# One step of a by-hand exponential moves between VectorE and GpSimd in an attention kernel

## The chip, the cores and the metric

The kernel runs on one core of one Trainium2 chip. The time is device time in microseconds (us) of one execution. A core has five engines with a queue each: TensorE (PE, matrix products; PEld are its weight loads), VectorE (DVE), ScalarE (ACT), GpSimd (POOL) and SyncE (SP, which here issues transfers only). Each works through its own queue in order, and they wait for each other by semaphores. An instruction that waits holds up all that stand behind it in its queue.

## What is computed

Attention with grouped heads: 8 batches, 512 positions, 32 query heads in 8 groups of 4 that share a key and a value head, 64 columns per head.

```python
scores = np.einsum('bhqd,bhkd->bhqk', Q, K_expanded) * scale
weights = np.exp(scores - np.max(scores, axis=-1, keepdims=True))
weights = weights / (np.sum(weights, axis=-1, keepdims=True) + 1e-10)
output = np.einsum('bhqk,bhkd->bhqd', weights, V_expanded)
```

## The kernel before

**Jobs.** The work is cut into 64 jobs (`NJOB`), one for each batch and key head. A job has two pairs of query heads (`NPAIR`), and for each pair 4 blocks of 128 keys by 2 heads: 16 blocks of 128 keys by 512 queries. For each block TensorE makes the transposed scores in PSUM (`scores`, L283), an engine takes the exponential into the float16 tile `pt`, and TensorE multiplies `pt` with V (`pv`, L376), whose 65th column of ones gives the sum of the weights. `norm` (L418, L423) takes the reciprocal `inv` of that sum and multiplies it into the output tile `o_sb`, which SP stores. The scores aren't shifted by their maximum; sums and values are checked for range, and a general path behind the fast one runs if a check fails.

**Who takes the exponential.** ScalarE does most blocks, two at a time (`act_tile`, L301, 128x1024). VectorE and GpSimd do `taken(j)` blocks of each job by hand: three in the jobs for which `WIDE(j)` holds (`j >= 4 and j % 4 < 3`, so three jobs running, then one with two blocks). In a three-block job ScalarE is left with 13 blocks: six full tiles and a half tile, which comes as the fifth. From job 4 on the jobs thus run in groups of four: a first, a middle and a last three-block job, then a two-block job. There are 15 such groups; the last one ends in job 63, which takes one block by hand.

**The exponential by hand.** Five instructions:
- `u` (L312, VectorE): scores times a factor plus an offset, rounded to int16, so that the bits are those of a float16 near the exponential. Two blocks come first, the third in a part of its own, one job ahead (`exp_d`).
- `f` (L324, VectorE): the ten mantissa bits of `u`.
- `g` (L329, `factor` in `exp_d2`): (f + a) * b. This is the correction's first step.
- `w` (L335, `product`, GpSimd): g times f, the correction itself.
- `pt` (L348, `exp_d4`, VectorE): u + w, in bits the weight. It is called in the next job.

Where `g` runs is set by `odd` in `exp_d2`. Before, `odd` holds for the middle and the last three-block job: there g is VectorE's, in all other jobs GpSimd's. In the middle one `exp_d2` returns g and w as `rest`, which the job's loop calls further down, behind the third `u` of the next job; in the last one g is issued at once, behind f and ahead of the copy of the transposes.

**Order of a job** (the loop over j from 1 to 62, by hand, no scheduler): ScalarE tile 0, first `u`, tile 1, pv of the previous job's first pair in two halves with tile 2 between, `norm`, tile 3; then the half tile and the transposes of the queries of job j + 2 (L215) in the two banks of a fresh `d_ps`; `exp_d4` of the previous job; `exp_d2` of this one; the copy of the transposes (`qt`, L220); pv of the previous job's second pair in parts between tiles 5 and 6, with the third `u` of the next job; `rest`; `norm`. Every engine sees its own instructions in that order.

**Buffers.** PSUM has two `s_ps` tiles for ScalarE's scores, one `d_ps` (scores for VectorE, or transposes) and one `pv`. So pv of a pair can start only when `o_sb` of the pair before has read `pv`, and the next `s_ps` scores stand behind it in TensorE's queue. `u`, `f`, `g`, `w` have two buffers each. GpSimd also issues the loads of Q, K and V (L114 to L142), at the start of a job; the first and the two-block jobs have some, the middle and the last none.

Of the kernel before, what the change touches and what calls it, by code (L numbers as in the profile page):

```python
# [40 lines left out]
WIDE = lambda j: j >= 4 and j % 4 < 3  # L41
# [26 lines left out]
def fast_path(ctx, tc, Q, K, V, out, flag, ident):  # L68
# [78 lines left out]
    def d_tile():  # L147
        return d_pool.tile([128, 2, S], FP32, name="d_ps")
# [3 lines left out]
    def first_k(gp, swap, bank):  # L152
        half_bank = bank.bitcast(BF16)[:, 0:S]
        ps = half_bank.rearrange("p (sc c) -> p sc c", sc=SC)
        h = 2 * gp
        done = []
        for sc in range(SC):
            if swap:
                for half, g in ((0, 1), (64, 0)):
                    done.append(nc.tensor.transpose(  # L160
                        ps[half:half + 64, sc, :], kn[0][:, sc, h + g, :], ident
                    ))
            else:
                done.append(nc.tensor.transpose(ps[:, sc, :], kn[0][:, sc, h:h + 2, :], ident))
        return done, lambda: nc.vector.tensor_copy(
            out=kt_first[:, gp, swap, :], in_=half_bank
        )
# [22 lines left out]
    def dma_k(b, lo=0):  # L190
        kt[b] = kt_pool.tile([128, 2, GP, S], BF16, name="kt")
        for sc in range(SC):
            nc.sync.dma_start_transpose(
                out=kt[b][:, 0, lo:, sc * 128:(sc + 1) * 128],
                in_=kn[b][:, sc, 2 * lo:, :].rearrange("p g d -> p (g d)"),
            )
        for to, of in ((0, 64), (64, 0)):
            nc.sync.dma_start(out=kt[b][to:to + 64, 1, lo:, :], in_=kt[b][of:of + 64, 0, lo:, :])
# [27 lines left out]
    def piece(bank, done, read):  # L226
        copy = read()
        for other, written, taken_out in pieces:
            if other != bank:
                for this in done:  # L230
                    apart(this, taken_out)
                for before in written:
                    apart(copy, before)
        pieces.append((bank, done, copy))

    def check_v(b, sc):
        n = b * SC + sc
        nc.vector.tensor_reduce(  # L238
            out=okv[:, n:n + 1], in_=vt[b % 2][:, sc, :, 0:D], op=ALU.max, axis=AX.XY,
            apply_absolute_value=True,  # L240
        )
# [4 lines left out]
    def taken(j):  # L246
        return 1 if j == NJOB - 1 else 3 if WIDE(j) else 2
# [14 lines left out]
    for b in range(B):  # L262
        span = range(max(3, 8 * b + 1), min(8 * b + 9, NJOB - 3))
        two = [j for j in span if not WIDE(j)]
        odd = [j for j in span if WIDE(j) and not WIDE(j + 1)]
# [25 lines left out]
    def open_job(j):  # L291
        pt = pt_pool.tile([128, NPAIR, SC, 2, S], FP16, name="pt")
        jobs.setdefault(j, {}).update(pt=pt, pv={})

    def act_tile(j, n, spare=None):
        group = act_tiles(j)[n]
        i, kc, lo = group[0]
        ps = s_pool.tile([128, 2, S], FP32, name="s_ps") if spare is None else spare
        for _, _, m in group:
            scores(j, ps[:, m, :], i, kc, m)  # L300
        return nc.scalar.activation(  # L301
            out=jobs[j]["pt"][:, i, kc, lo:, :], in_=ps[:, lo:, :], func=EXP, scale=scale
        )

    def exp_d(j, lo, hi, ps, other=None):
        st = jobs.setdefault(j, {})
        if "u" not in st:
            for name, dtype in (("u", I16), ("f", I16), ("g", BF16), ("w", BF16)):
                st[name] = dve_pool.tile([128, 3, S], dtype, name=name + "16")[:, 0:taken(j), :]
        for n in range(lo, hi):  # L310
            apart(scores(j, ps[:, n - lo, :], DPAIR, *divmod(d_block(j) + n, 2)), other)
        return lambda: nc.vector.tensor_scalar(  # L312
            out=st["u"][:, lo:hi, :], in0=ps[:, 0:hi - lo, :], scalar1=A_U, scalar2=B_U,
            op0=ALU.mult, op1=ALU.add,
        )
# [3 lines left out]
    def exp_d2(j, engine=None):  # L319
        st = jobs[j]  # L320
        by_bits = engine is None
        engine = engine or nc.gpsimd
        odd = WIDE(j) and WIDE(j - 1)
        nc.vector.tensor_single_scalar(  # L324
            out=st["f"], in_=st["u"], scalar=1023, op=ALU.bitwise_and
        )

        def factor():
            (nc.vector if odd else engine).tensor_scalar(  # L329
                out=st["g"], in0=st["f"], scalar1=-EXP_F1,  # L330
                scalar2=EXP_K * 2.0 ** (24 * by_bits), op0=ALU.add, op1=ALU.mult,
            )

        def product():
            engine.tensor_tensor(  # L335
                out=st["w"], in0=st["g"], in1=st["f"].bitcast(FP16) if by_bits else st["f"],
                op=ALU.mult,
            )

        if odd and WIDE(j + 1):  # L340
            return lambda: (factor(), product())
        factor()
        return product() if by_bits else product
# [20 lines left out]
    def pv(j, i, lo, hi):  # L364
        st = jobs[j]
        u, g = divmod(j, 2)
        b, gp = divmod(u, GP)
        if lo == 0:

            t = d_tile() if (j, i) == (NJOB - 1, 0) else pv_tile()  # L370
            t = t.rearrange("p m (qc c) -> p m qc c", qc=SC)
            st["pv"][i] = t[:, :, :, 0:D + 1]
        order = blocks(j, i)
        for n in range(lo, hi):
            kc, m, qc = order[n]
            nc.tensor.matmul(  # L376
                st["pv"][i][:, m, qc, :],
                st["pt"][:, i, kc, m, qc * 128:(qc + 1) * 128],
                vt[b % 2][:, kc, 2 * gp + g, :],
                start=(n < 2 * SC and qc == 0),  # L380
                stop=(n >= len(order) - 2 * SC and qc == SC - 1),
            )
# [11 lines left out]
    def check_sums():  # L394
        while full:
            k, n = full.pop()
            cols = n * 2 * SC
            flat = invs.pop(k).rearrange("p s m qc -> p (s m qc)")[:, 0:cols]
            in_bounds((ok[:, 0:cols], ok[:, 0:cols]), flat, ok[:, 0:cols])
# [161 lines left out]
    act_tile(0, 3)  # L561
    act_tile(0, 4)
    exp_d2(0)
    bank = pv_tile()
    piece(0, *trans_q(1, bank[:, 0, :], 0, 1))
# [6 lines left out]
    for j in range(1, NJOB - 1):  # L572
        last = j - 1
        u, g = divmod(j, 2)
        b, gp = divmod(u, GP)
        open_job(j)
        if j == 1:
            nc.gpsimd.tensor_copy(out=gate, in_=jobs[0]["pt"][0:1, 0, SC - 1, 0, 0:1])
        for load, *of in LOADS.get(j, ()):
            load(*of)  # L580
        if j == 1:
            dma_k(0, 2)
        if gp == 2 and g == 0 and b + 1 < B:
            dma_k(b + 1)

        cut = (11, 19) if taken(j) < 3 else (4, 18) if taken(last) < 3 else (4, 16)
        act_tile(j, 0)
        if j == 1:
            piece(1, *first_k(1, 0, bank[:, 1, S // 2:]))
        exp_d(j, 0, 2, d_tile())()  # L590
        act_tile(j, 1)
        if j < 4 or j % 4 == 0:
            check_sums()
        if (j, 0) in CHECKS:
            check_v(*CHECKS[j, 0])
        pv(last, 0, 0, 16)
        act_tile(j, 2)
        pv(last, 0, 16, 32)
        norm(last, 0)
        act_tile(j, 3)  # L600

        reads = []
        bank = d_tile()
        beside = act_tile(j, 4, bank) if taken(j) > 2 else None

        ahead = (j + 1,) if j < 2 else (3, 4) if j == 2 else (j + 2,)
        for n, to in enumerate(ahead):
            if to < NJOB:
                reads.append(trans_q(to, bank[:, n, :], other=beside)[1])
        if j == 1:  # L610
            reads.append(first_k(1, 1, bank[:, 1, :])[1])
        exp_d4(last)
        rest = exp_d2(j)
        copies = [read() for read in reads]
        if taken(j) == 2:
            act_tile(j, 4)
        pv(last, 1, 0, cut[0])
        act_tile(j, 5)
        if beside:
            pv(last, 1, *cut)  # L620
        if taken(j + 1) > 2:
            exp_d(j + 1, 2, taken(j + 1), bank[:, 1:2, :], copies[0])()
        if rest:
            rest()
        if (j, 1) in CHECKS:
            check_v(*CHECKS[j, 1])
        if not beside:
            pv(last, 1, *cut)
        act_tile(j, 6)
        pv(last, 1, cut[1], 32)  # L630
        norm(last, 1)
        del jobs[last]

    j, last = NJOB - 1, NJOB - 2
# [144 lines left out]
```

## Time and profile before

| | us |
|---|---|
| median of 3 runs | 410.0 (409.52 to 410.16) |
| the profiled execution | 410.13 |
| its span, first to last instruction | 408.3 |
| ScalarE busy | 397.2 |
| TensorE busy | 374.7 |
| VectorE busy | 370.2 |
| GpSimd busy | 257.4 |

The granted TensorE clock was 0.998 of full speed. In the timeline's lines the first number is the start in us from the beginning of the span, the second the length in us; then come the engine, the line of the kernel, the operation, the tile written and the tiles read, shapes, and how many instructions were merged into the line. In square brackets stands the idle time of the engine just before, and what ended it. The records of one engine overlap a little, since the next instruction is taken up before the last result has landed, so lengths can't simply be added; starts and ends can be compared. Records of GpSimd are rough.

### The profile page before, as it was taken

To read this page: it belongs to the slowest core of one execution; us is meant where nothing else is said; L and a number is where in the kernel's file an instruction comes from. 1 tells how busy PE (TensorE), PEld (TensorE's weight loads), DVE (VectorE), ACT (ScalarE), POOL (GpSimd) and SP (SyncE) were. 2 spreads that over 40 slices of the span, in tenths; PEclk is the share of its full clock that TensorE was granted. 3 is DMA by queue.
4 is the path that set the end of the run, shared out by engine and by line. 5 is a ranking of instruction groups with operands and counts; after the bars stand their busy time and mean duration, and the time that the engine had idled before them with its cause. 6 is when DMAs were issued, how large, how long until landed. Compare 5 with 4: busy or idle time off the path is not lost.

```text
span 408.3 us, 13010 instructions
## 1 busy us (share of the span) xinstructions
PE 374.7 (92%) x5670; PEld 228.2 (56%) x5670; DVE 370.2 (91%) x653; ACT 397.2 (97%) x455; POOL 257.4 (63%) x151
## 2 busy tenths in 40 slices
PE   7999999998999999999998999999999999999975
PEld 3565565564655655555555555555555555555543
DVE  3788999999999998999989999899999999899985
ACT  5999999999999999999999999999999999999995
POOL 9858476675666666485674766567475684565552
PEclk9999999999999999999999999999999999999999
DMA  9989999699955999289890999919996399322205
GB/s 144 158 199 181 128 289 214 185 141 133 285 152 147 148 251 178 106 178 133 268 217 36 212 107 293 219 63 182 153 258 177 119 127 215 114 104 104 105 18 195
DMA packets 82893, 67.73 MB, mean 166 GB/s; under 512 B 52752, under 2 KB 57872, under 8 KB 82832
## 3 DMA queue, kind: packets, MB, share of 16 engines
q0 software_dynamic: 45072, 24.91, 62.1%
q1 hardware_dynamic: 37216, 41.75, 37.3%
q8 instruction: 45, 0.74, 0.8%
q10 hardware_dynamic: 544, 0.20, 0.2%
q14 instruction: 16, 0.13, 0.1%
HBM read 50.33 MB, written 33.55 MB: 205 GB/s over the span
## 4 chain that ended last, share of the span: by engine, by line
DVE 40%; PE 30%; ACT 27%; issue 3%; ACTq 0%; DVEq 0%
ACT pt L301 27%; PE pv L376 15%; DVE o_sb L423 11%; PE s_ps L283 11%; DVE u L312 6%; DVE pt L348 6%; DVE qt L220 5%; DVE g L329 4%; DVE inv L418 2%; DVE okv L238 2%; PE d_ps L215 2%; DVE f L324 2%; PE d_ps L283 1%; PE s_ps L512 1%; DVE inv_last L418 0%
## 5 line engine op out<-in xcount | busy, mean ns | idle before, releaser
L301 ACT ACTIVATE pt<-s_ps 128x1024 f16<-128x1024 f32 x403 | 381.3, 1094 | 2.5 <-PE s_ps L283 1.9
L335 POOL TENSOR_TENSOR w<-g,f 128x1536 bf16<-128x1536 bf16 (+1 forms) x63 | 177.4, 2816 | 88.8 <-DVE g L329 86.1
L376 PEld LDWEIGHTS <-pt 128*128 128x128 f16 x4096 | 142.4, 98 | 89.0 <-issue 42.9
L376 PE MATMUL pv<-v,pt 128*128 128x65 bf16 x4064 | 179.3, 195 | 10.9 <-DVE o_sb L423 10.1
L283 PE MATMUL s_ps<-qt,kt 64*128 64x512 bf16 x751 | 152.6, 384 | 9.0 <-ACT pt L301 7.2
L312 DVE TENSOR_SCALAR u<-d_ps 128x1024 int16<-128x1024 f32 (+1 forms) x109 | 107.8, 989 | 0.3
L423 DVE TENSOR_TENSOR o_sb<-pv,inv 128x512 f32<-128x512 f32 x121 | 83.6, 691 | 4.2
L283 PEld LDWEIGHTS <-kt 64*128 64x128 bf16 x960 | 50.0, 93 | 53.3 <-issue 29.3
L329 POOL TENSOR_SCALAR g<-f 128x1024 bf16<-128x1024 int16 (+1 forms) x33 | 40.6, 1230 | 53.3 <-DVE f L324 53.3
L283 PE MATMUL d_ps<-qt,kt 64*128 64x512 bf16 x209 | 56.9, 376 | 5.9 <-DVE qt L220 2.3
L348 DVE TENSOR_TENSOR pt<-u,w 128x1536 uint16<-128x1536 int16 (+1 forms) x64 | 55.3, 864 | 0.0
L418 DVE RECIPROCAL inv<-pv 128x8 f32<-128x8 f32 x121 | 24.8, 205 | 19.5 <-PE pv L376 17.4
L220 DVE COPY qt<-d_ps 128x1024 bf16<-128x1024 bf16 x62 | 42.2, 682 | 0.0
L215 PEld LDWEIGHTS <-q_nat 128*128 128x128 bf16 x508 | 28.5, 97 | 23.2 <-issue 23.2
L215 PE MATMUL d_ps<-ident,q_nat 128*128 128x128 bf16 x496 | 38.3, 221 | 0.0
L324 DVE TENSOR_SCALAR f<-u 128x1536 int16<-128x1536 int16 (+1 forms) x64 | 32.7, 512 | 0.0
L301 ACT ACTIVATE pt<-d_ps 128x512 f16<-128x512 f32 x45 | 31.0, 688 | 0.0
L238 DVE TENSOR_REDUCE okv<-v 128x1 f32<-128x512 bf16 x32 | 21.6, 675 | 0.0
L329 DVE TENSOR_SCALAR g<-f 128x1536 bf16<-128x1536 int16 (+1 forms) x31 | 16.9, 546 | 0.6
L142 POOL DMA_DIRECT2D q_nat<-in_Q_dram x19 | 15.4, 812 | 0.1
L283 PE MATMUL s_ps<-qt,kt_first 64*128 64x512 bf16 x56 | 11.1, 399 | 1.8 <-ACT pt L301 1.6
L127 POOL DMA_DIRECT2D v<-in_V_dram x7 | 12.3, 1759 | 0.0
(58 smaller groups left out, 55.1 us busy)
## 6 DMA issues: line engine op xcount, KB each, us to landing
out_dram<-o_sb SPq DMA_DIRECT2D x31, 1024.0 KB, 5.8
q_nat<-in_Q_dram POOLq DMA_DIRECT2D x14, 1024.0 KB, 11.5
k_nat<-in_K_dram POOLq DMA_DIRECT2D x7, 512.0 KB, 7.6
v<-in_V_dram POOLq DMA_DIRECT2D x7, 512.0 KB, 14.6
kt<-kt SPq DMA_DIRECT2D x14, 256.0 KB, 4.3
q_nat<-in_Q_dram POOLq DMA_DIRECT2D x3, 512.0 KB, 7.8
out_dram<-o_sb SPq DMA_DIRECT2D x4, 256.0 KB, 2.2
kt<-k_nat SPq DMA_TRANSPOSE x32, 10.3
```

The costliest lines, as they stand in the source:

```text
L215: nc.tensor.transpose(ps[:, i, sc, :], qn[u // 2][:, sc, h:h + 2, :], ident),
L220: return done, lambda: apart(nc.vector.tensor_copy(out=qt[u][:, g, lo:hi, :], in_=ps[:, lo:hi, :, :].rearrange("p i sc c -> p i (sc c)")), ...
L283: return nc.tensor.matmul(ps, keys[64 * m:64 * m + 64, g if u == 0 else g ^ m, kc * 128:(kc + 1) * 128], qt[u][64 * m:64 * m + 64, g, i, : ...
L301: return nc.scalar.activation(out=jobs[j]["pt"][:, i, kc, lo:, :], in_=ps[:, lo:, :], func=EXP, scale=scale)
L312: return lambda: nc.vector.tensor_scalar(out=st["u"][:, lo:hi, :], in0=ps[:, 0:hi - lo, :], scalar1=A_U, scalar2=B_U, op0=ALU.mult, op1=AL ...
L324: nc.vector.tensor_single_scalar(out=st["f"], in_=st["u"], scalar=1023, op=ALU.bitwise_and)
L329: (nc.vector if odd else engine).tensor_scalar(out=st["g"], in0=st["f"], scalar1=-EXP_F1, scalar2=EXP_K * 2.0 ** (24 * by_bits), op0=ALU.a ...
L335: engine.tensor_tensor(out=st["w"], in0=st["g"], in1=st["f"].bitcast(FP16) if by_bits else st["f"], op=ALU.mult,)
L348: nc.vector.tensor_tensor(out=st["pt"][:, DPAIR, :, :, :].rearrange("p kc m q -> p (kc m) q")[:, d_block(j):d_block(j) + n, :].bitcast(U16 ...
L376: nc.tensor.matmul(st["pv"][i][:, m, qc, :], st["pt"][:, i, kc, m, qc * 128:(qc + 1) * 128], vt[b % 2][:, kc, 2 * gp + g, :], start=(n < 2 ...
L418: nc.vector.reciprocal(out=inv, in_=sums[:, :, :, D:D + 1])
L423: nc.vector.tensor_tensor(out=osb[u][:, :, h:h + 2, :].rearrange("p qc m d -> p m qc d"), in0=sums[:, :, :, 0:D], in1=inv[:, :, :, None].t ...
```

## The change

g moves to GpSimd in the middle three-block job, at once behind f, with w behind it. In the last three-block job it stays on VectorE, but behind the copy of the transposes. `rest` is called directly behind the copies.

```diff
@@ exp_d2
-        odd = WIDE(j) and WIDE(j - 1)
+        odd = WIDE(j) and not WIDE(j + 1)
...
-        if odd and WIDE(j + 1):
+        if odd:
             return lambda: (factor(), product())
         factor()
         return product() if by_bits else product
@@ the loop over the jobs
         rest = exp_d2(j)
         copies = [read() for read in reads]
+        if rest:
+            rest()
         if taken(j) == 2:
             act_tile(j, 4)
         pv(last, 1, 0, cut[0])
...
         if taken(j + 1) > 2:
             exp_d(j + 1, 2, taken(j + 1), bank[:, 1:2, :], copies[0])()
-        if rest:
-            rest()
         if (j, 1) in CHECKS:
```

## The prediction

> **What bounds the kernel now.** I read the page's busy table first, then the timeline of each engine over one period of four jobs (204 to 230 us; by the first and last run of the sum below, 42.25 and 362.50 in 13 steps, it repeats every 24.6 us), and the waits noted in it.
>
> ```profile
> PE 374.7 (92%) x5670; PEld 228.2 (56%) x5670; DVE 370.2 (91%) x653; ACT 397.2 (97%) x455; POOL 257.4 (63%) x151
> ```
>
> ScalarE (ACT) has nearly no idle time. So the question is whether it runs at its own rate throughout. Its timeline, merged into runs of full tiles (x6, x13) and half tiles (x1), answers that; columns are start, length, engine, line:
>
> ```profile
> 208.60 0.71 ACT L301 ACTIVATE pt<-d_ps 128x512 f16<-128x512 f32 x1
> 209.07 5.73 ACT L301 ACTIVATE pt<-s_ps 128x1024 f16<-128x1024 f32 x6
> 214.53 0.77 ACT L301 ACTIVATE pt<-d_ps 128x512 f16<-128x512 f32 x1
> 215.00 5.94 ACT L301 ACTIVATE pt<-s_ps 128x1024 f16<-128x1024 f32 x6
> 220.84 0.59 ACT L301 ACTIVATE pt<-d_ps 128x512 f16<-128x512 f32 x1
> 221.31 12.03 ACT L301 ACTIVATE pt<-s_ps 128x1024 f16<-128x1024 f32 x13
> ```
>
> The records overlap, so I count from end to end. The half tile ends at 209.31 and the six tiles behind it at 214.80: 5.49 us, 0.915 each. The 13 tiles from 221.43 to 233.34 take 11.91, 0.916 each. That is ScalarE's own rate. The six between them, from 215.30 to 220.94, take 5.64: **0.15 us is lost, once in four jobs**, in the run that goes from the middle to the last of the three three-block jobs. TensorE (PE) shows what came late:
>
> ```profile
> 217.18 0.39 PE L283 MATMUL s_ps<-qt,kt 64*128 64x512 bf16 x2
> 217.96 0.67 PE L376 MATMUL pv<-v,pt 128*128 128x65 bf16 x16 [0.38 <-DVE o_sb L423]
> 218.56 0.39 PE L283 MATMUL s_ps<-qt,kt 64*128 64x512 bf16 x2
> ```
>
> TensorE works in order. Its pv matmuls wait 0.38 us for VectorE's (DVE) division o_sb, which empties the one pv buffer, and the next scores (218.56) stand behind them. VectorE is one unbroken queue there:
>
> ```profile
> 213.98 0.95 DVE L348 TENSOR_TENSOR pt<-u,w 128x1536 uint16<-128x1536 int16 x1
> 214.85 0.55 DVE L324 TENSOR_SCALAR f<-u 128x1536 int16<-128x1536 int16 x1
> 215.31 0.68 DVE L220 COPY qt<-d_ps 128x1024 bf16<-128x1024 bf16 x1
> 215.91 0.68 DVE L312 TENSOR_SCALAR u<-d_ps 128x512 int16<-128x512 f32 x1
> 216.51 0.55 DVE L329 TENSOR_SCALAR g<-f 128x1536 bf16<-128x1536 int16 x1
> 216.98 0.20 DVE L418 RECIPROCAL inv<-pv 128x8 f32<-128x8 f32 x1
> 217.21 0.69 DVE L423 TENSOR_TENSOR o_sb<-pv,inv 128x512 f32<-128x512 f32 x1
> ...
> 220.44 0.95 DVE L348 TENSOR_TENSOR pt<-u,w 128x1536 uint16<-128x1536 int16 x1
> 221.31 0.55 DVE L324 TENSOR_SCALAR f<-u 128x1536 int16<-128x1536 int16 x1
> 221.89 0.56 DVE L329 TENSOR_SCALAR g<-f 128x1536 bf16<-128x1536 int16 x1
> ...
> 223.20 0.69 DVE L423 TENSOR_TENSOR o_sb<-pv,inv 128x512 f32<-128x512 f32 x1
> ...
> 226.40 0.95 DVE L348 TENSOR_TENSOR pt<-u,w 128x1536 uint16<-128x1536 int16 x1
> ```
>
> The f at 214.85 is the middle job's, the one at 221.31 the last's. g is the step that the change moves: in the middle job it stands directly ahead of the late inv and o_sb.
>
> **The change part by part.** The order of instructions of both kernels, set side by side, is the same on PE, ACT and SP. VectorE loses 15 g (the middle jobs), and has g behind the copy instead of ahead of it in the last jobs; GpSimd (POOL) gains 15 g, each directly ahead of its w.
>
> *Step 1, g leaves VectorE in the middle job.* From g to inv is 0.47 us (216.51 to 216.98), so inv could start at 216.51. It also needs the pv matmuls ahead of it:
>
> ```profile
> 215.87 0.66 PE L376 MATMUL pv<-v,pt 128*128 128x65 bf16 x16
> ```
>
> They end at 216.53; with 0.06 for the signal, as between o_sb's end (217.90) and pv (217.96), that is 216.59. o_sb follows 0.23 later, at 216.82, and pv 0.75 behind that (as 217.21 to 217.96): at 217.57, which is when TensorE is free (217.18 + 0.39). Gain: **0.39 us on TensorE**, and its wait is gone. The next scores come at 218.17 instead of 218.56. ScalarE lacked 0.15, so its loss disappears with 0.24 to spare. It can't gain more, for it then runs at 0.916 per tile. What is late next on ScalarE in this stretch is ScalarE itself.
>
> *Step 2, g arrives on GpSimd.* GpSimd's rows, and the f of the first three-block job ahead of them:
>
> ```profile
> 208.60 0.55 DVE L324 TENSOR_SCALAR f<-u 128x1536 int16<-128x1536 int16 x1
> ```
>
> ```profile
> 209.25 1.46 POOL L329 TENSOR_SCALAR g<-f 128x1536 bf16<-128x1536 int16 x1 [2.12 <-DVE f L324]
> 210.80 3.09 POOL L335 TENSOR_TENSOR w<-g,f 128x1536 bf16<-128x1536 bf16 x1
> 217.14 3.09 POOL L335 TENSOR_TENSOR w<-g,f 128x1536 bf16<-128x1536 bf16 x1 [3.25 <-DVE g L329]
> ```
>
> The first job shows the very sequence: g 0.65 us behind the start of f, w 1.55 later, 3.09 long. For the middle job: g at 215.50, w at 217.05, done at 220.14. GpSimd waited 3.25 us there, so g's 1.46 costs its queue nothing, and w starts 0.09 earlier than now, for before it had to wait for VectorE to come to g. The cost of the handoff back to VectorE is bounded by the first job: from f (208.60) to the L348 that needs w (213.98) is 5.38, and no idle time is noted ahead of that L348, so w did not hold it. So the middle's L348 is possible at 214.85 + 5.38 = 220.23 at the latest, and not before 220.14. Apart from w, VectorE reaches it 0.39 earlier than now, at 220.05. I take 220.20: **VectorE now waits some 0.15 us for w, but is still 0.24 earlier than now**. Behind the waiting L348 stand f, copy, g, inv and o_sb of the last job, and pv behind those; all come earlier than now, so the new wait costs nothing. If that cover were gone (L348 later than now), they would be late, see the rivals.
>
> The Trainium skill (Perfetto Trace Analysis, "GPSIMD Engine Instruction") calls GpSimd's recorded spans unreliable and wants start-to-start times. By that the 220.14 would fall and the 220.23, which hangs on VectorE's starts alone, would stay; the sum is the same.
>
> *Step 3, g behind the copy in the last job.* L348 at 220.20 puts f at 221.07, copy at 221.53 (0.46 behind f, as 214.85 to 215.31), g at 222.13, inv at 222.60, o_sb at 222.83: 0.37 earlier than 223.20, of which 0.13 is the gap from f to g (0.58) shrunk to that of f to copy (0.46). pv behind it gains as much; ScalarE loses nothing there now (the 13 tiles at 0.916), so it brings nothing. g ends at 222.69, w starts 0.08 behind it (as 217.06 to 217.14) at 222.77 and is done at 225.86. Its L348 moves from 226.40 to about 226.03, so w is in time by 0.17. If that cover went, L348 could slip by 0.37 before it came later than now.
>
> The load of q_nat behind w in GpSimd's queue goes out some 0.2 later than now:
>
> ```profile
> 225.63 0.82 POOL L142 DMA_DIRECT2D q_nat<-in_Q_dram  x1
> ```
>
> It fills a buffer that is transposed seven jobs later, so nothing. SP's stores follow o_sb, which comes earlier. `rest()` at its new place issues only this g and w.
>
> *The sum.* The lossy run of six appears 14 times, first and last:
>
> ```profile
> 42.25 5.93 ACT L301 ACTIVATE pt<-s_ps 128x1024 f16<-128x1024 f32 x6
> ...
> 362.50 5.94 ACT L301 ACTIVATE pt<-s_ps 128x1024 f16<-128x1024 f32 x6
> ```
>
> One of the 14 is torn by another gap (below). 13 x 0.145 = 1.9 us.
>
> ```profile
> 96.13 0.65 PE L376 MATMUL pv<-v,pt 128*128 128x65 bf16 x16 [0.71 <-issue]
> ```
>
> ```profile
> 97.14 1.02 ACT L301 ACTIVATE pt<-s_ps 128x1024 f16<-128x1024 f32 x1 [0.66 <-PE s_ps L283]
> ```
>
> Here TensorE stopped for 0.71 us without waiting for any instruction ("issue"), and may do so at the same moment again: between 0 and 0.15, I take 0.1. In the fifteenth group, at the end, more is lost at the same place:
>
> ```profile
> 391.10 0.67 PE L376 MATMUL pv<-v,pt 128*128 128x65 bf16 x16 [0.70 <-DVE o_sb L423]
> 392.13 1.95 ACT L301 ACTIVATE pt<-s_ps 128x1024 f16<-128x1024 f32 x2 [0.67 <-PE s_ps L283]
> ```
>
> g stands ahead of that o_sb too; without it pv comes 0.47 earlier and ScalarE's 0.67 idle falls to 0.2. A few hundredths may be lost again behind w; I take 0.4. Sum: 1.9 + 0.1 + 0.4 = **2.4 us**. After the last tile the tail is unchanged. The profiled execution took 410.13 (span 408.3 and 1.8 around it), so 407.7; the median of the three timed runs is 0.13 lower: **407.6**.
>
> **The rivals.**
>
> *ScalarE is faster than its ends show, so the whole 0.39 counts.* Then 15 x 0.39 = 5.9, 404. For it: by starts instead of ends, the lossy six take 5.84 us (215.00 to 220.84) and the six before them 5.46 (209.07 to 214.53), 0.38 less, just what TensorE waited. Against it: the ends stay at 0.915 over 6 and 13 tiles, however early the tiles start. The Trainium skill (ScalarE: Activation LUTs, "What ACT_TABLE_LOAD costs") gives 0.833 ns per element, an estimate of 0.85 us for 1024; by that the larger gain would be open. The trace has 0.916, and that decides.
>
> *w takes the place of g, no change.* If L348 came at about 220.58, the last job's o_sb would be so late that ScalarE loses there the 0.145 that it gained: 410. It needs a handoff 0.35 longer than the 5.38 of the first job, with the same instructions beside it but for one reduction, which stands beside the middle's w already now.
>
> *Slower: g is held by VectorE's copy on GpSimd.* If g could start only when the copy ends (215.31 + 0.68 = 215.99), w would end at 220.63 and L348 start at about 220.68. From L348 to o_sb is 0.87 + 0.46 + 0.60 + 0.47 + 0.23 = 2.63 us. o_sb at 223.20 costs ScalarE nothing now; I take that as its limit, so ScalarE, 0.145 earlier, needs it by about 223.06, and begins to lose when L348 passes 220.43, and the change is a loss past 220.58. At 220.68 it loses 0.25 and gains 0.145: 0.1 x 15 = 1.6, 411.6. Against it: in the first job g starts at 209.25, inside the copy that follows f there too, and takes 1.46. The Trainium skill (SBUF — State Buffer, "Who interferes with whom") has VectorE's two-port instructions lock GpSimd out for their whole length, and a copy can be one if its operands are in SBUF. By that rule this copy, which reads PSUM, holds nothing; the trace agrees with the 1.46.
>
> **How the numbers follow.** Chances: the forecast 0.74, a larger gain 0.08, no change 0.10, slower 0.08. The forecast's own spread is 407.0 to 408.4: a stop like the one at 97 us may come or go (0.7 us), and the three runs shown lie 0.6 apart. To hold 8 in 10 the range reaches halfway into the neighbours: 406.2 to 409.6. The bound for faster and slower is 0.2% (0.8 us), about what a measurement of this kernel can tell from no change: faster 0.82, same 0.10, slower 0.08.
>
> **What would show it.** Right: in the middle job GpSimd's g about 0.65 behind f and w about 5.3 behind f at its end; VectorE's L348 of the middle with a small wait for w; no wait of pv for the o_sb behind the moved step; runs of six full tiles that all take 5.5 from end to end; VectorE's busy time down by about 7 to 8 us and GpSimd's up by 22 (15 x 1.46). Wrong: g on GpSimd longer than 1.5 or started after the copy; L348 of the middle waiting more than 0.4; pv of the last job waiting for o_sb longer than now; or six tiles at 5.64 still, with the scores in time, which would say that the loss was never o_sb's.

## The result, and the profile after

| | before | after |
|---|---|---|
| median, us (6 runs each) | 409.86 (409.08 to 410.20) | 406.27 (405.84 to 406.44) |
| profiled execution / its span | 410.13 / 408.3 | 406.28 / 404.5 |

The ratio is 0.9913, with a 95% interval of 0.9901 to 0.9926: 3.0 to 4.1 us less. The forecast was 407.6, 2.4 us less than the 410.0 it started from. The direction held. The range, 406.2 to 409.6, held by 0.07 us, and the size of 2.4 us was too small by about a third of the 3.6 measured.

The busy table of the page after:

```profile
PE 376.3 (93%) x5670; PEld 230.1 (57%) x5670; DVE 364.0 (90%) x638; ACT 395.1 (98%) x455; POOL 279.8 (69%) x166
```

GpSimd is busy 22.4 us longer (22 were forecast), VectorE 6.2 us less (7 to 8 were forecast). The same period of four jobs on ScalarE, in the kernel after:

```profile
206.56 0.78 ACT L301 ACTIVATE pt<-d_ps 128x512 f16<-128x512 f32 x1
207.03 5.80 ACT L301 ACTIVATE pt<-s_ps 128x1024 f16<-128x1024 f32 x6
212.56 0.77 ACT L301 ACTIVATE pt<-d_ps 128x512 f16<-128x512 f32 x1
213.03 5.79 ACT L301 ACTIVATE pt<-s_ps 128x1024 f16<-128x1024 f32 x6
218.60 0.72 ACT L301 ACTIVATE pt<-d_ps 128x512 f16<-128x512 f32 x1
```

From end to end: 207.34 to 212.83 and 213.33 to 218.82, 5.49 us for both runs of six. The 0.15 us that the second one lost is gone. On TensorE the pv matmuls (215.58) and the scores behind them (216.19) no longer wait:

```profile
215.21 0.39 PE L283 MATMUL s_ps<-qt,kt 64*128 64x512 bf16 x2
215.58 0.67 PE L376 MATMUL pv<-v,pt 128*128 128x65 bf16 x16
216.19 0.39 PE L283 MATMUL s_ps<-qt,kt 64*128 64x512 bf16 x2
```

VectorE's timeline from the f of the middle job to the L348 of the last:

```profile
212.88 0.55 DVE L324 TENSOR_SCALAR f<-u 128x1536 int16<-128x1536 int16 x1
213.34 0.69 DVE L220 COPY qt<-d_ps 128x1024 bf16<-128x1024 bf16 x1
213.94 0.68 DVE L312 TENSOR_SCALAR u<-d_ps 128x512 int16<-128x512 f32 x1
214.59 0.21 DVE L418 RECIPROCAL inv<-pv 128x8 f32<-128x8 f32 x1
214.83 0.69 DVE L423 TENSOR_TENSOR o_sb<-pv,inv 128x512 f32<-128x512 f32 x1
...
217.46 0.69 DVE L423 TENSOR_TENSOR o_sb<-pv,inv 128x512 f32<-128x512 f32 x1
218.20 0.96 DVE L348 TENSOR_TENSOR pt<-u,w 128x1536 uint16<-128x1536 int16 x1
219.07 0.55 DVE L324 TENSOR_SCALAR f<-u 128x1536 int16<-128x1536 int16 x1
219.54 0.68 DVE L220 COPY qt<-d_ps 128x1024 bf16<-128x1024 bf16 x1
220.15 0.55 DVE L329 TENSOR_SCALAR g<-f 128x1536 bf16<-128x1536 int16 x1
220.61 0.20 DVE L418 RECIPROCAL inv<-pv 128x8 f32<-128x8 f32 x1
220.85 0.69 DVE L423 TENSOR_TENSOR o_sb<-pv,inv 128x512 f32<-128x512 f32 x1
...
224.05 0.95 DVE L348 TENSOR_TENSOR pt<-u,w 128x1536 uint16<-128x1536 int16 x1
```

And GpSimd's:

```profile
213.52 1.47 POOL L329 TENSOR_SCALAR g<-f 128x1536 bf16<-128x1536 int16 x1 [1.60 <-DVE f L324]
215.07 3.10 POOL L335 TENSOR_TENSOR w<-g,f 128x1536 bf16<-128x1536 bf16 x1
220.77 3.10 POOL L335 TENSOR_TENSOR w<-g,f 128x1536 bf16<-128x1536 bf16 x1 [2.61 <-DVE g L329]
```

L348 at 218.20 starts 0.74 behind the start of o_sb (217.46); in the kernel before it was 0.61 (219.83 to 220.44). These 0.13 us are the new wait for w, whose record ends at 218.17. The wait is there, and ScalarE loses nothing behind it: the 13 tiles behind 218.60 run at 0.917 each. What the wait costs is tested below, in the run without g.

### The profile page after: what moved, and what is told of

Same layout as the page of the kernel before. It is cut to its first block, busy times and chain, and to the rows that moved or that the text cites. A ratio compares the mean times of both kernels' runs of the same rounds, so it can differ in the third digit from the quotient of the medians.

```text
span 404.5 us, 12995 instructions
## 1 busy us (share of the span) xinstructions
PE 376.3 (93%) x5670; PEld 230.1 (57%) x5670; DVE 364.0 (90%) x638; ACT 395.1 (98%) x455; POOL 279.8 (69%) x166
## 4 chain that ended last, share of the span: by engine, by line
ACT 42%; DVE 21%; PE 19%; POOL 15%; issue 2%; ACTq 0%; DVEq 0%
ACT pt L301 42%; POOL w L335 10%; PE pv L376 9%; PE s_ps L283 8%; DVE pt L348 7%; POOL g L329 5%; DVE o_sb L423 4%; DVE f L324 3%; DVE qt L220 3%; DVE g L329 2%; DVE inv L418 1%; PE d_ps L283 1%; DVE u L312 1%; PE s_ps L512 1%; DVE okv L238 0%
## 5 line engine op out<-in xcount | busy, mean ns | idle before, releaser
L329 POOL TENSOR_SCALAR g<-f 128x1536 bf16<-128x1536 int16 (+1 forms) x48 | 62.7, 1305 | 72.8 <-DVE f L324 72.7
L283 PEld LDWEIGHTS <-kt 64*128 64x128 bf16 x960 | 52.3, 93 | 57.4 <-issue 31.5
L348 DVE TENSOR_TENSOR pt<-u,w 128x1536 uint16<-128x1536 int16 (+1 forms) x64 | 55.5, 867 | 0.8
L301 ACT ACTIVATE pt<-d_ps 128x512 f16<-128x512 f32 x45 | 34.5, 767 | 0.0
L329 DVE TENSOR_SCALAR g<-f 128x1536 bf16<-128x1536 int16 (+1 forms) x16 | 8.6, 535 | 0.1
```

The lines of the kernel that those rows point to most:

```text
L283: return nc.tensor.matmul(ps, keys[64 * m:64 * m + 64, g if u == 0 else g ^ m, kc * 128:(kc + 1) * 128], qt[u][64 * m:64 * m + 64, g, i, : ...
L301: return nc.scalar.activation(out=jobs[j]["pt"][:, i, kc, lo:, :], in_=ps[:, lo:, :], func=EXP, scale=scale)
L329: (nc.vector if odd else engine).tensor_scalar(out=st["g"], in0=st["f"], scalar1=-EXP_F1, scalar2=EXP_K * 2.0 ** (24 * by_bits), op0=ALU.a ...
L348: nc.vector.tensor_tensor(out=st["pt"][:, DPAIR, :, :, :].rearrange("p kc m q -> p (kc m) q")[:, d_block(j):d_block(j) + n, :].bitcast(U16 ...
```

## The experiments

The theory: in the middle job g stood ahead of an o_sb for which TensorE waited; its removal brings the gain, g costs nothing on GpSimd, and the order in the last job does nothing. Rivals: the last job's order carries a part; VectorE's amount of work counts, not the place; the new wait for w costs something. All times are medians, and the kernel before was timed with each group of runs on the same chip (409.81, 409.55 and 410.11).

**Part one alone.** In the kernel after, the last job's g goes back ahead of the copy:

```diff
-        if odd:
-            return lambda: (factor(), product())
         factor()
         return product() if by_bits else product
```

> Part one alone: g of the middle job on GpSimd; in the last job g stays on VectorE ahead of the copy, as before. Theory (the loss is g ahead of o_sb in the middle job): nearly the whole gain, 3.0 to 3.8 us less than before, and every run of six full ScalarE tiles at 5.5 us from end to end. Rival (the order in the last job carries a part of it): 2 us less or below.

Measured: 406.79, ratio 0.9918 (0.9898 to 0.9938), 3.0 us less than before. Its run of six:

```profile
212.83 0.77 ACT L301 ACTIVATE pt<-d_ps 128x512 f16<-128x512 f32 x1
213.31 5.79 ACT L301 ACTIVATE pt<-s_ps 128x1024 f16<-128x1024 f32 x6
```

213.60 to 219.10, 5.50 us. No run of six loses anything but those of jobs 30 and 46, where TensorE paused (0.2 and 0.6), and the one in the last group (0.70, with the whole change 0.60). So part one brings the gain, to within the interval.

**Part two alone.** `odd` as before, so that the middle job's g stays on VectorE at its old place; only the last job's goes behind the copy:

```diff
         copies = [read() for read in reads]
+        if rest and not WIDE(j + 1):
+            rest()
...
-        if rest:
+        if rest and WIDE(j + 1):
             rest()
```

> Part two alone: g of the last job behind the copy; in the middle job g stays on VectorE, at its old place. Theory: no change, within 0.4 us of before, and the run of six at 5.64 in each group as before. Rival (part two carries a part): 0.8 to 2 us less.

Measured: 409.60, ratio 0.9984 (0.9967 to 1.0001): no change that this measurement can tell. TensorE and ScalarE look as before:

```profile
218.52 0.67 PE L376 MATMUL pv<-v,pt 128*128 128x65 bf16 x16 [0.39 <-DVE o_sb L423]
```

```profile
215.09 0.77 ACT L301 ACTIVATE pt<-d_ps 128x512 f16<-128x512 f32 x1
215.57 5.94 ACT L301 ACTIVATE pt<-s_ps 128x1024 f16<-128x1024 f32 x6
```

215.86 to 221.51 is 5.65. In the last job o_sb does come earlier, 2.63 us behind L348 (221.01 to 223.64) instead of 2.76 (220.44 to 223.20). That is the 0.13 that the prediction put down to the order, and it is worth nothing, since nobody was late by it.

**The place, not the amount of work.** The kernel before, with the middle job's g still on VectorE, behind the o_sb:

```diff
-        if rest:
-            rest()
...
         norm(last, 1)
+        if rest:
+            rest()
```

> The kernel before, with g of the middle job still on VectorE, but behind the o_sb that it held up. Theory (its place counts, on both ends): o_sb comes 0.4 earlier, but w starts near 218.06 instead of 217.14 in the period shown, L348 0.75 later, so the loss moves to the last job and grows: slower by 5 to 10 us. Rival (VectorE's amount of work counts, which is the same): no change.

Measured: 419.12, ratio 1.0224 (1.0200 to 1.0248), 9.3 us slower than before, with the same work on every engine. o_sb was early as expected, 1.97 behind f (218.57 to 220.54) instead of 2.36, but w came late:

```profile
224.90 0.96 DVE L348 TENSOR_TENSOR pt<-u,w 128x1536 uint16<-128x1536 int16 x1 [0.64 <-POOL w L335]
```

The loss on ScalarE comes in the two-block job behind, where it waits for scores:

```profile
228.22 1.02 ACT L301 ACTIVATE pt<-s_ps 128x1024 f16<-128x1024 f32 x1 [0.20 <-PE s_ps L283]
229.44 2.85 ACT L301 ACTIVATE pt<-s_ps 128x1024 f16<-128x1024 f32 x3 [0.20 <-PE s_ps L283]
```

Losses here and below are counted from the end of one tile to the end of the next and compared with 0.917 for a full tile and 0.490 for a half one: some 0.70 to 0.80 us are lost in each two-block job from 11 on, and the loss in the last three-block job falls from 0.13 and more to some 0.07. So neither of these two places for g on VectorE is free: ahead of o_sb it delays TensorE now, behind it w delays TensorE one job later.

**What g costs on GpSimd.** The kernel after with g left out in the middle job; w is made from f alone, so the correction of these blocks is left out:

```diff
-                out=st["w"], in0=st["g"], in1=...
+                out=st["w"], in0=st["f"].bitcast(FP16) if skip else st["g"], in1=...
...
-        factor()
+        if not skip:
+            factor()
```

> The kernel after, without g in the middle job (w is made from f alone; the correction of these blocks is left out). Theory (g costs nothing on GpSimd): no faster than the kernel after, 3.0 to 3.8 us less than before. Rival (the new wait of VectorE for w costs 0.15 us in each group): 2 us faster than the kernel after, 5 to 6 less than before.

Measured: 406.20, ratio 0.9901 (0.9884 to 0.9919); the kernel after had 406.27 and, repeated, 406.26. w is then 1.5 us earlier and VectorE never waits for it, and it brings nothing: the rival's 2 us are excluded, and ScalarE's losses are those of the kernel after but for TensorE's pause in job 30 (0.55 and 0.45). To within that, g on GpSimd and the new wait are free.

**How late may w be?** Dummy fills on GpSimd between g and w of the middle job, in the kernel after, one or two of them:

```diff
         factor()
+        if by_bits and WIDE(j) and WIDE(j - 1) and WIDE(j + 1):
+            for _ in range(1):    # or 2
+                nc.gpsimd.memset(idle, 0.0)
         return product() if by_bits else product
```

> The kernel after, with one dummy fill of a 128x128 float32 tile on GpSimd between g and w of each middle job (0.28 us in the page, some 0.33 from start to start), so that w and the L348 behind it come 0.33 later. By the prediction's limit (L348 may slip 0.23 before ScalarE loses, 0.38 before the change is a loss): ScalarE loses 0.1 in each of 14 groups, so 1.4 us slower than the kernel after, near 407.7. Rival (the slack is larger than that): as the kernel after, 406.3.

> The same with two dummy fills, w later by some 0.66. By the prediction's limit ScalarE loses 0.43 in each group: 14 x 0.43 = 6 us slower than the kernel after, near 412, slower than before. Rival: slower than the kernel after by less than half of that.

The fills were shorter than I had put them. From the start of f to L348 it is 5.32 us in the kernel after; with one fill 5.46 (212.74 to 218.20), with two 5.73 (214.19 to 219.92): L348 slipped by 0.14 and 0.41, not 0.33 and 0.66. With two fills:

```profile
214.19 0.55 DVE L325 TENSOR_SCALAR f<-u 128x1536 int16<-128x1536 int16 x1
...
219.92 0.96 DVE L352 TENSOR_TENSOR pt<-u,w 128x1536 uint16<-128x1536 int16 x1 [0.44 <-POOL w L336]
```

```profile
219.93 0.71 ACT L302 ACTIVATE pt<-d_ps 128x512 f16<-128x512 f32 x1
220.40 12.28 ACT L302 ACTIVATE pt<-s_ps 128x1024 f16<-128x1024 f32 x13
```

One fill: 406.72, ratio 0.9933 (0.9918 to 0.9947), and no loss in any of the first 14 groups. Two: 408.80, ratio 0.9977 (0.9963 to 0.9992); the 13 tiles take 220.64 to 232.68, 12.04 instead of 11.92, so 0.12 us is lost, and 0.11 to 0.15 in the other groups (in job 14's a pause of TensorE instead), now in the two-block job. The prediction's limit of 0.23 would have given 0.41 - 0.23 = 0.18. The limit measured is 0.41 - 0.13 = 0.28. With two fills most of the gain is eaten; by the prediction's point of no gain, 0.38, nothing would have been left of it, and 0.75 us was (409.55 to 408.80). The stated times, 407.7 and 412, missed because the slip was mis-sized.

**The rest of the loss in the last group.** After the change ScalarE still loses 0.6 us in job 62. The final range check (two products over the sums, two reductions, a verdict: 0.93 us) stands ahead of the L348 in job 61. I moved all of it behind the u in job 63:

```diff
     exp_d(j, 0, 1, d_tile())()
     act_tile(j, 1)
+    verdict()    # the whole check, out of norm
```

> The kernel after, with the final range check of VectorE (0.93 us in job 61, ahead of its L348) moved into VectorE's idle time in job 63. Theory (in the last group ScalarE still loses 0.6 us because that check delays L348, u and o_sb): 0.4 to 0.6 us faster than the kernel after, 405.7 to 405.9. Rival (the loss there has another cause): as the kernel after.

Measured: 406.98, ratio 0.9934 (0.9920 to 0.9949), no better than the kernel after. The loss in job 62 went from 0.60 to nothing, so its cause was right, but 0.58 appeared in job 63. VectorE's and GpSimd's timelines show what held there:

```profile
393.23 2.08 DVE L387 SCALAR_TENSOR_TENSOR ok<-inv,ok 128x72 f32<-128x72 f32 x2
395.22 0.18 DVE L443 TENSOR_REDUCE vmax<-okv 128x1 f32<-128x32 f32 x1
```

```profile
391.85 3.09 POOL L335 TENSOR_TENSOR w<-g,f 128x1536 bf16<-128x1536 bf16 x1 [2.14 <-DVE g L329]
```

The two products take 2.08 us, against 0.49 at their old place; the first takes 1.81 of it and ends at 395.04, 0.1 behind the end of w (394.94). So I cut the check in pieces, and put only the reductions beside w:

```diff
     exp_d(j, 0, 1, d_tile())()
     act_tile(j, 1)
+    extremes()    # the two reductions
...
     check_sums()
+    verdict()     # the product of the two
     product = exp_d2(j, nc.vector)
```

> The kernel after, with the final range check cut up: its two products over the sums stay at their place in job 61, the two reductions go into VectorE's idle time in job 63, the verdict behind L348 there, when GpSimd's w is done. In the run with the whole check in job 63 the first product started at 393.23 beside a w (391.85 to 394.94) and ended at 395.04 instead of after 0.22. Theory (a VectorE instruction with two operands in SBUF is held until GpSimd's w is done): the pieces take 0.2 to 0.3 us each, ScalarE's loss in job 62 falls from 0.60 to some 0.2, none appears in job 63, 0.3 to 0.4 us faster than the kernel after. Rival (the long product had another cause): a piece in job 63 takes over 1 us again, and nothing is gained.

```profile
393.13 0.17 DVE L445 TENSOR_REDUCE vmax<-okv 128x1 f32<-128x32 f32 x1
393.23 0.27 DVE L446 TENSOR_REDUCE okmin<-ok 128x1 f32<-128x128 f32 x1
...
396.20 0.15 DVE L449 SCALAR_TENSOR_TENSOR okall<-vmax,okmin 128x1 f32<-128x1 f32 x1
```

Measured: 406.16, ratio 0.9910 (0.9892 to 0.9929). ScalarE's loss in job 62 fell from 0.60 to 0.08, and none came in job 63. In time that can't be told from the kernel after on the same chip:

> The kernel after itself, on the same chip as the run beside it. 3.4 to 3.8 us less than before; TensorE's pause of 0.3 to 0.8 us without a wait falls into another job than in the first profile, if it isn't set by the program.

Measured: 406.26, ratio 0.9912 (0.9897 to 0.9928). The forecast 0.3 to 0.4 us isn't shown by the time. The profiled execution of the cut-up check has a TensorE pause of 0.8 us without a wait, in job 30; that of the repeated kernel after lost 0.2 in that job. The pause thus didn't move to another job, as expected if it weren't set by the program, but it changed in length, and half a microsecond of gain can hide in the spread of such pauses.

**Four late tiles on ScalarE.** Before the change ScalarE also lost 0.13 to 0.20 us at the first tiles of jobs 7, 23, 39 and 55, though their scores were there. To see whether that goes by ScalarE's count of instructions, 16 tiny copies were put at its start, in the kernel before:

```diff
+    for _ in range(16):
+        nc.scalar.activation(out=nudge[:, 1:2], in_=nudge[:, 0:1], func=COPY)
     nc.scalar.activation(out=qn[0][:, half:, 0:2, :], in_=qf[:, half:, :, :], func=COPY)
```

> The kernel before, with 16 tiny copies on ScalarE at the start. In before, the ScalarE record numbers 63, 191, 319 and 447 start late, 128 apart; these are the first tiles of jobs 7, 23, 39 and 55. Theory (it goes by the count of ScalarE's instructions): the late tiles are those some 16 records earlier, in jobs 5, 21, 37 and 53. Rival (it goes by the place in the program): jobs 7, 23, 39 and 55 again. The start is 2 to 4 us longer.

Measured: 412.98, one run. The loss went two jobs up, to jobs 5, 21, 37 and 53 (0.17, 0.14, 0.14, 0.14), and is gone from the four others; the late tiles are records 63, 191, 319 and 447 of ScalarE again (counted from 0, and with ScalarE's waits and other records of its sequencer, eight records a job). The first of them, with the 16 copies:

```profile
38.90 0.75 ACT L301 ACTIVATE pt<-d_ps 128x512 f16<-128x512 f32 x1
39.38 5.94 ACT L301 ACTIVATE pt<-s_ps 128x1024 f16<-128x1024 f32 x6
...
51.34 0.59 ACT L301 ACTIVATE pt<-d_ps 128x512 f16<-128x512 f32 x1
51.82 12.03 ACT L301 ACTIVATE pt<-s_ps 128x1024 f16<-128x1024 f32 x13
```

The run of six into the middle job takes 5.67 (39.65 to 45.32) instead of the 5.49 that it takes elsewhere, and the 13 tiles behind take 11.92 (51.93 to 63.85). So it goes by the count of records, 128 from one to the next, and not by the place in the program.

## Why the prediction was right, and where it was too small

- **Step 1, g leaves VectorE**: right. Counted from the middle job's f, o_sb was forecast 1.97 behind it and came at 1.95, pv at 2.72 and came at 2.70. The loss in the runs of six, 0.13 to 0.17 in each of 13 groups (1.85 us in all), went to nothing but for the pause in job 30; forecast 1.9. The run of part one alone shows the gain with it, that of part two alone none.
- **Step 2, g on GpSimd**: right. g 0.64 behind f (0.65), w 2.19 (2.20), L348 5.32 (5.35, between 5.29 and 5.38). The new wait is 0.13 us (0.15), and free, as the run without g shows.
- **Step 3, the last job**: right. From L348 to o_sb 2.65 us (2.63); w ends at 223.87, 0.18 ahead of its L348 (0.17). It brings nothing that can be measured, as the run of part two alone shows.
- **The sum**: too small, and the largest term that was mis-sized is one put at nothing. The prediction looked at one run of 13 tiles, which ran at 0.916 each, and had ScalarE lose only in the runs of six. Four of the other such runs were longer before. One of them, in before and then in after, from the half tile ahead of it:

```profile
147.12 0.59 ACT L301 ACTIVATE pt<-d_ps 128x512 f16<-128x512 f32 x1
147.59 12.17 ACT L301 ACTIVATE pt<-s_ps 128x1024 f16<-128x1024 f32 x13
```

```profile
144.97 0.72 ACT L301 ACTIVATE pt<-d_ps 128x512 f16<-128x512 f32 x1
145.45 12.16 ACT L301 ACTIVATE pt<-s_ps 128x1024 f16<-128x1024 f32 x13
```

147.71 to 159.76 is 12.05; 145.69 to 157.61 is 11.92. The lengths look alike, and only the ends show it. These are the late tiles of jobs 7, 23, 39 and 55: together 0.60 us less. They start late after the change too, by 0.16 us in job 23 (0.17 before), but then it costs nothing, because of what the lost 0.15 had taken along. While its scores are there in time, ScalarE starts a tile ahead of the end of the one before, and by some 0.013 us more with each tile: the half tile's record is 0.72 us long after the change, where it was 0.59. A tile that starts late sets this lead back, and a next hiccup soon behind it is then paid nearly in full. Ahead of the late tile of job 23 the lead was 0.13 before the change and 0.14 of the 0.17 was lost; after it the lead was 0.26 and nothing was lost. The run with two fills separates the stall from its nearness: there the stall lies 26 tiles ahead of that late tile instead of five, the lead is back at 0.25, and the 0.16 costs nothing. That fits the 0.75 us of gain that this run keeps. So a single stall costs its own length and, if another hiccup comes soon, the cover of that one.
- **The last group**: 0.57 + 0.08 (jobs 62 and 60) instead of 0.4. What took the 0.08 in job 60 before the change was not looked into.
- **TensorE's pause near 96 us**: the 0.1 counted there came out as 0.9 in the two profiles, but 0.46 came back in job 30. In the other profiles such pauses add up to between 0 and 1 us, mostly in jobs 14 and 30. That is a spread between executions, and no gain of the change.
- **The tail**: it was to be unchanged. From the end of the last tile to the end of the span it is 0.18 us longer after (5.15 against 4.97), and so in the repeated profile; VectorE, TensorE and ScalarE do their last work at the same distances as before, and why the span ends later is open.

The parts that the change explains are 1.85 + 0.13 (the own loss of the group that TensorE's stop tore) + 0.60 + 0.65 = 3.2 us; the measured 3.0 to 4.1 agrees. The steps were right for the reason given, but that the range held was in part luck: the time lies outside the forecast's own spread of 407.0 to 408.4, and only the widening into the neighbours took it in.
- **The rivals.** *The whole 0.39 counts*: no; ScalarE's ends stay at 0.917 per tile throughout, and what was added is the four late tiles and the last group, not a faster ScalarE. The estimate of 0.85 us counted the 1024 elements alone: by the ends, 0.917 for 1024 and 0.490 for 512, an element takes 0.834 ns and each tile 0.063 us more, which makes up the 0.917, so that figure spoke for no larger gain. *w takes the place of g*: it doesn't here, but its price was nearly right; with L348 0.41 later most of the gain is gone. *g is held by the copy*: no; g starts at 213.52, inside the copy (213.34 to 214.03), and takes 1.47.

## What to carry to other kernels

On an engine that is busy 97% of the span, compare the ends of its records, run by run, with its own rate: the missing tenths show which wait is worth removing, and all equal runs have to be looked at, not one. A step on a crowded queue has a place as well as a length: look up who waits for what stands right behind it, and who waits for its own result, and take the engine where both have slack. An engine that starts each step ahead of the end of the last holds a lead that covers a hiccup; a stall removed shortly ahead of one gives that cover back too.

## What the runs showed of the hardware that I had not expected

- **VectorE held by GpSimd.** As the run with the whole check in job 63 showed, a product of two SBUF operands, 0.22 us by itself, took 1.81 us beside GpSimd's w, until 0.1 us behind w's end, while two reductions with one operand, in the run with the cut-up check, took 0.17 and 0.27 beside the w at that place, as elsewhere. The kernel before has it in small: the check's first product on 128x128 takes 0.37 to 0.38 us in the six places where it starts some 0.23 ahead of the end of a w, and 0.28 in the one without a w (378.86). The Trainium skill (SBUF — State Buffer, "Who interferes with whom") says that a VectorE instruction with two SBUF inputs contends with a GpSimd instruction that reads SBUF, that the shared ports are an exclusive lock, and that the order of issue decides who is blocked. The runs agree with it. That L348, with two SBUF operands as well, never lay beside a w follows from its needing w.
- **ScalarE starts late every 128 records** (63, 191, 319, 447): by 0.16 to 0.24 us in before and after, and by 0.28 to 0.31 in the run with the 16 copies, where the late tile stands right behind a wait of its sequencer and a lead of 0.23 didn't cover it. It was seen at these two places in the program, the second in a single run; the cause beyond the count stays open.
- **TensorE pauses** without a wait, which cost ScalarE 0.2 to 0.9 us in a profile, mostly in jobs 14 and 30, and differ from one execution of a kernel to the next. They limit the difference that one profile can show here; their cause is open.
